# One TensorE loop body per unit, with the spread of v as an inner loop, in an attention-times-value kernel

## The chip, the cores and the metric

The kernel runs on one core of a Trainium2 chip. The metric is device time in microseconds (us) of one execution, given as the median of several runs. The engines of the core are TensorE (PE; its weight loads are listed apart as PEld), VectorE (DVE), ScalarE (ACT), GpSimd (POOL) and SyncE (SP). Sixteen DMA engines move data between the chip's memory and the on-chip memories; here GpSimd issues most transfers and SyncE a few.

## What is computed

```
batch, n_heads, seq, head_dim = 8, 12, 1024, 64
np.einsum('bhqs,bhsd->bhqd', attn_weights, v).astype(np.float32)
```

There are 96 heads. For each one, a 1024 x 1024 matrix of attention weights is multiplied with a 1024 x 64 matrix v. Inputs and output are float32. The attention weights alone are 402.7 MB, so nearly all of the traffic is reading them once.

## The kernel before

**Units.** Four heads are taken together (24 such groups, `NV`), and a group's attention weights come in two loads of 1024 x 2048 values, called units here (48, `NU`). GpSimd's DMA converts a unit to bf16 while it loads it into one of two buffers `abf[0]` and `abf[1]`: even units (i = 0) into the first, odd units into the second. A buffer is free for the next load but one as soon as TensorE has transposed its content.

**What TensorE does for a unit**, in this order (`pe_unit`, line 199):

- Transposes (`transpose_g`, line 139, recorded as L144): 16 groups `g` of four 128 x 128 transposes; two bf16 values travel as one float32 word. They go through four banks of the accumulation memory, and VectorE (10 of 16 groups) and ScalarE (6 of 16) copy them to `at` (`copy_g`, L277). A group waits for the copy of the group four before it (`s_cp`).
- Spread, for even units only (`spread_v`, line 154, L161): the four heads' v lies in `vr` with rows over partitions, eight heads on 128 partitions, 16 partitions each. Matmuls with a 0/1 matrix `spread` bring it into the layout that the product needs: for each of the four heads, eight matmuls of 512 columns are summed in one bank. The operands are slices of 32 partitions (`rows`), and two heads whose slices differ are interleaved. Four copies of this code exist, one for each place that a group can have in `vr`, and three nested tests choose one. VectorE and ScalarE cast two banks each to `vbf` (`spread_copy`, L250).
- Transposing back (`transpose_back`, line 171, L174) of the product of the unit before, from `ot`; ScalarE copies it to the output buffer `osb` (`back_copy`, L258).
- Product (`multiply`, line 184, L189): for each of four heads and two halves, eight matmuls that accumulate `vbf` times `at`. VectorE and ScalarE copy the result to `ot` (`product`, L289).

TensorE's loop runs 24 times, and its body holds both units of a group, each written out, plus the four copies of the spread. After the loop one more transposing back is written out.

**What sets the order.** Every engine runs its instructions in program order, and engines wait for each other by semaphores with counts worked out by hand. GpSimd's queue is a fixed list: for each unit n it waits until all transposes of n are done (`s_t[True]` at line 396; the last group, 15, is one of VectorE's) and issues the load of unit n + 2. Ahead of some even units it waits until a spread is done (`s_sp`, line 394) and issues a load of v for the next groups; the attention load behind it in the list then waits too. Stores of finished output are issued by GpSimd in two bursts (`BURSTS`, after groups 8 and 16), twice at its end, and three times by SyncE at the end; SyncE also passes on, through `s_half`, that a burst has been stored or that the second half of one of the last two units has landed. Those last two units are loaded in halves. TensorE looks at `s_half` ahead of group 8 of each unit.

Of the kernel before, what the change touches and what calls it, by code (L numbers as in the profile page):

```python
# [10 lines left out]
def kernel(  # L11
# [76 lines left out]
    def count_of(g):  # L88

        return sum(on_dve(x) == on_dve(g) for x in range(g + 1))  # L90

    PER_DVE = sum(on_dve(g) for g in range(G))
    PER_ACT = G - PER_DVE

# [15 lines left out]
    bank = [nc.alloc_psum_tensor(f"bank{i}", [P, 512], fp32).ap() for i in range(8)]  # L110
    pt = [b.rearrange("p (k j) -> p k j", k=KW) for b in bank[:4]]
    po = bank[4:6]
    px = bank[6:8]

# [7 lines left out]
    s_t = {True: sem("s_t_dve"), False: sem("s_t_act")}  # L122
# [4 lines left out]
    s_last, s_ot, s_vbf = sem("s_last"), sem("s_ot"), sem("s_vbf")  # L127
# [8 lines left out]
    with tc.tile_critical(sync_engine=mybir.EngineType.Pool, no_gpsimd_drain=True):  # L136
        pe = nc.tensor

        def transpose_g(a, g, n):
            if g >= 4:  # L140
                pe.wait_ge(s_cp[g - 4], n)
            words = a[:, g].bitcast(fp32).rearrange("p (c k) -> p k c", k=KW)
            for k in range(KW):
                last = pe.matmul(  # L144
                    out=pt[g % 4][:, k],
                    lhsT=words[:, k],
                    rhs=ident,
                    is_transpose=True,
                    start=(k == 0),
                    stop=(k == KW - 1),  # L150
                )
            last.then_inc(s_t[on_dve(g)])

        def spread_v(n, banks):

            for pair in ((0, 2), (1, 3)):
                for b in range(VB):
                    for h in pair:
                        j = n % 2 * VH + h
                        rows = ds(j * (P // V8) // VR * VR, VR)  # L160
                        last = pe.matmul(  # L161
                            out=banks[h],
                            lhsT=spread[rows, j, ds(VB - 1 - b, P)],
                            rhs=vr[rows, n // 2, b],
                            start=(b == 0),
                            stop=(b == VB - 1),
                        )
                        if b == VB - 1:
                            last.then_inc(s_sp)

        def transpose_back():
            for j0 in range(0, GH, 4):
                for j in range(4):
                    last = pe.matmul(  # L174
                        out=px[j0 // 4][:, ds(j * P, P)],
                        lhsT=ot[:, j0 + j],
                        rhs=ident,
                        is_transpose=True,
                        start=(j == 0),
                        stop=(j == 3),  # L180
                    )
                last.then_inc(s_back)

        def multiply(outs, h, half):

            n = 0
            for kw in range(KW):
                for par in range(2):
                    last = pe.matmul(  # L189
                        out=outs,  # L190
                        lhsT=vbf[:, 2 * kw + par, h],
                        rhs=at[:, ds(half * GH, GH), kw, ds(h * VP, VP), par],
                        start=(n == 0),
                        stop=(n == SB - 1),
                    )
                    n += 1
            return last

        def pe_unit(i, n, both, loaded, it):

            pe.wait_ge(*loaded)
            for g in range(G):
                if g == GH:
                    pe.wait_ge(s_half, n)
                transpose_g(abf[i], g, n)
            pe.wait_ge(s_ot, both)
            if i == 0:
                pe.wait_ge(s_vr, it)
                which = pe.snap((it - 1) % V_AT_ONCE)
                with pe.If(which > 1):  # L210
                    with pe.If(which > 2):
                        spread_v(3, po + px)
                    with pe.Else():
                        spread_v(2, po + px)
                with pe.Else():
                    with pe.If(which > 0):
                        spread_v(1, po + px)
                    with pe.Else():
# [3 lines left out]
            pe.wait_ge(s_last, both)  # L222
            for hp in range(2):
                for h in range(2):
                    for half in range(2):
                        outs = po[hp][ds(half * D, D), ds(h * GH * VP, GH * VP)]
                        last = multiply(outs, 2 * hp + h, half)
                last.then_inc(s_m)

        pe.wait_ge(s_const, 4)  # L230
        with nc.Fori(1, NV + 1, 1, engines=(PE,)) as it:
            loaded = pe.snap(it * 16)
            second = pe.snap(it * 2)
            first = pe.snap(second - 1)
            both = pe.snap(it * 4)
# [230 lines left out]
```

## Time and profile before

| quantity | value |
|---|---|
| median of 3 runs | 1050.6 us (1050.5 to 1050.88) |
| the profiled execution's own time | 1050.13 us |
| its span, from first to last instruction | 1048.7 us |
| mean granted TensorE clock | 0.876 |
| read from and written to the chip's memory | 427.82 MB and 25.17 MB |
| transposes (L144), PE busy | 430.3 us of 3072 matmuls |
| product (L189), PE busy | 226.3 us of 3072 matmuls |
| spread (L161), PE busy | 87.0 us of 768 matmuls |
| transposing back (L174), PE busy | 61.9 us of 392 matmuls |
| PE idle before transposes, until a load of attention weights | 186.5 us |
| loads of attention weights, of a whole unit | 46, median 29.4 us from issue to landing |
| loads of v of 2048 KB | 5, median 15.7 us from issue to landing |

A page of the profile gives each engine's busy time, the span in 40 slices with the share of time that the DMA engines moved data, the groups of equal instructions with busy time, mean duration and the idle time ahead of them, and the chain of waits that ended last. Asked for a stretch of time, the trace gives the same figures for that stretch, or the instructions in order (the timeline). Sizes of loads are those written on the chip, in bf16, half of what is read. Busy time on an engine that others wait for counts; idle time on an engine that nobody waits for costs nothing.

### The profile page before, as it was taken

The numbers are of one execution on the slowest core, as the hardware profiler recorded it, in microseconds if no ns is written. First come the engines' busy times: TensorE is split into PE (matmuls) and PEld (weight loads), VectorE is DVE, ScalarE is ACT, GpSimd is POOL, SyncE is SP. The second block draws the span as 40 slices with busy tenths as digits, with TensorE's granted clock in tenths as the row PEclk, the third lists the DMA queues.
The fourth block names the chain that finished last, engine by engine and source line by source line (L and its number), as shares of the span: only waits on it lengthen the run. The fifth ranks groups of instructions, "written<-read, shape, count | busy, mean of one in ns | idle before, by whom it ended". The sixth has DMA issues, their size and how long they took to land.

```text
span 1048.7 us, 17363 instructions
## 1 busy us (share of the span) xinstructions
PE 795.5 (76%) x7304; PEld 708.5 (68%) x7304; DVE 389.4 (37%) x584; ACT 469.5 (45%) x590; POOL 36.9 (4%) x68
## 2 busy tenths in 40 slices
PE   0978789479889493888949789858577784988994
PEld 0777688368778383777848678657567674877883
DVE  1443344234435151343415344324234332433542
ACT  0445355344545261354536355344335443545553
POOL 1000000000000000000000000000000000000000
PEclk9989799798999696889879889889878987888997
DMA  9999999999999999999999999999999999999999
GB/s 216 226 219 219 216 212 215 220 219 217 220 215 209 220 220 376 220 217 211 211 224 220 216 220 212 210 221 220 318 238 217 212 210 224 220 216 219 209 214 402
DMA packets 10662, 239.68 MB, mean 229 GB/s; under 512 B 1056, under 2 KB 1056, under 8 KB 1184
## 3 DMA queue, kind: packets, MB, share of 16 engines
q0 software_dynamic: 10080, 232.26, 98.9%
q1 hardware_dynamic: 576, 7.34, 1.7%
q8 instruction: 3, 0.05, 0.0%
q14 instruction: 3, 0.02, 0.0%
HBM read 427.82 MB, written 25.17 MB: 432 GB/s over the span
## 4 chain that ended last, share of the span: by engine, by line
DMA 71%; PE 26%; issue 1%; POOL 1%; ACT 0%; DVE 0%; ACTq 0%; SPq 0%; POOLq 0%
DMA abf<-in_attn_weights_dram 63%; PE bank L144 22%; DMA out_dram<-osb 8%; PE bank L161 3%; PE bank L189 1%; PE bank L174 0%; POOL vr L350 0%; ACT osb L258 0%; DVE osb L258 0%; ACT vbf L250 0%; POOL abf L344 0%; ACT ot L289 0%; POOL out_dram L358 0%; ACTq L258 0%; SPq L420 0%
## 5 line engine op out<-in xcount | busy, mean ns | idle before, releaser
L144 PE MATMUL bank<-ident,abf 128*128 128x128 f32 x3072 | 430.3, 307 | 210.1 <-DMA abf<-in_attn_weights_dram 186.5
L144 PEld LDWEIGHTS bank<-ident,abf 128*128 128x128 f32 x3072 | 420.4, 212 | 221.9 <-DMA abf<-in_attn_weights_dram 193.8
L277 DVE COPY at<-bank 128x1024 bf16<-128x1024 bf16 x480 | 319.7, 689 | 400.1 <-PE bank L144 397.9
L277 ACT COPY at<-bank 128x1024 bf16<-128x1024 bf16 x288 | 287.8, 1012 | 327.2 <-PE bank L144 327.2
L189 PE MATMUL bank<-at,vbf 128*64 128x256 bf16 x3072 | 226.3, 286 | 0.0
L189 PEld LDWEIGHTS bank<-at,vbf 128*64 128x64 bf16 x3072 | 204.1, 111 | 19.6 <-issue 6.3
L258 ACT COPY osb<-bank 64x512 f32 (+1 forms) x194 | 112.4, 580 | 28.2 <-PE bank L174 25.7
L289 DVE COPY ot<-bank 128x512 f32<-128x512 f32 x48 | 33.2, 691 | 208.6 <-PE bank L189 208.6
L161 PE MATMUL bank<-vr,spread 32*128 32x512 bf16 x768 | 87.0, 375 | 0.5 <-issue 0.2
L289 ACT COPY ot<-bank 128x512 f32<-128x512 f32 x48 | 28.1, 585 | 130.5 <-PE bank L189 130.5
L174 PE MATMUL bank<-ident,ot 128*128 128x128 f32 x392 | 61.9, 309 | 29.4 <-ACT vbf L250 28.7
L174 PEld LDWEIGHTS bank<-ident,ot 128*128 128x128 f32 x392 | 50.8, 158 | 41.5 <-ACT vbf L250 40.5
L161 PEld LDWEIGHTS bank<-vr,spread 32*128 32x128 bf16 x768 | 35.3, 93 | 43.7 <-issue 1.6
L250 ACT CAST vbf<-bank 128x512 bf16<-128x512 f32 x48 | 25.8, 588 | 74.3 <-PE bank L161 74.3
L344 POOL DMA_DIRECT2D abf<-in_attn_weights_dram x50 | 26.9, 538 | 813.2 <-PE bank L144 812.3
L250 DVE CAST vbf<-bank 128x512 bf16<-128x512 f32 x48 | 30.9, 686 | 29.0 <-PE bank L161 29.0
L277 ACT ACT_TABLE_LOAD x12 | 15.4, 1283 | 6.5 <-DMA osb<-in_v_dram 6.3
L350 POOL DMA_DIRECT2D vr<-in_v_dram x6 | 4.0, 674 | 134.5 <-PE bank L161 134.5
L358 POOL DMA_DIRECT2D out_dram<-osb x5 | 3.1, 619 | 7.5 <-ACT osb L258 7.5
L325 DVE MEMSET ident<- 128x128 f32 x1 | 0.2, 165 | 6.3 <-DMA osb<-in_v_dram 6.3
L258 DVE COPY osb<-bank 64x512 f32<-64x512 f32 x2 | 1.4, 689 | 3.0 <-PE bank L174 3.0
L332 DVE CAST vr<-osb 128x1024 bf16<-128x1024 f32 x2 | 2.2, 1137 | 0.0
(9 smaller groups left out, 5.1 us busy)
## 6 DMA issues: line engine op xcount, KB each, us to landing
abf<-in_attn_weights_dram POOLq DMA_DIRECT2D x46, 4096.0 KB, 29.4
vr<-in_v_dram POOLq DMA_DIRECT2D x5, 2048.0 KB, 15.7
out_dram<-osb POOLq DMA_DIRECT2D x1, 8192.0 KB, 39.3
abf<-in_attn_weights_dram POOLq DMA_DIRECT2D x4, 2048.0 KB, 23.4
out_dram<-osb POOLq DMA_DIRECT2D x3, 2048.0 KB, 34.1
out_dram<-osb SPq DMA_DIRECT2D x3, 2048.0 KB, 14.3
out_dram<-osb POOLq DMA_DIRECT2D x1, 4096.0 KB, 42.8
osb<-in_v_dram SPq DMA_DIRECT2D x1, 1024.0 KB, 5.2
```

What stands on the lines that cost most here:

```text
L144: last = pe.matmul(out=pt[g % 4][:, k], lhsT=words[:, k], rhs=ident, is_transpose=True, start=(k == 0), stop=(k == KW - 1),)
L161: last = pe.matmul(out=banks[h], lhsT=spread[rows, j, ds(VB - 1 - b, P)], rhs=vr[rows, n // 2, b], start=(b == 0), stop=(b == VB - 1),)
L174: last = pe.matmul(out=px[j0 // 4][:, ds(j * P, P)], lhsT=ot[:, j0 + j], rhs=ident, is_transpose=True, start=(j == 0), stop=(j == 3),)
L189: last = pe.matmul(out=outs, lhsT=vbf[:, 2 * kw + par, h], rhs=at[:, ds(half * GH, GH), kw, ds(h * VP, VP), par], start=(n == 0), stop=(n ...
L250: copy(out=vbf[:, :, h], in_=ps.rearrange("p (k d) -> p k d", k=SB)).then_inc(s_vbf)
L258: last = copy(out=rows[ds(n // 2 % 2 * HP, HP), ds(pp * 2 * G + n % 2 * G, G)].rearrange("p (half j) d -> p j half d", half=2)[:, ds(4 * k ...
L277: ins = copy(out=at[:, g].rearrange("c k j two -> c (k j two)"), in_=bank[g % 4].bitcast(bf16),)
L289: copy(out=ot.rearrange("c j (pp h p) -> c h j pp p", pp=2, h=VH)[:, ds(2 * e, 2)], in_=po[e].rearrange("c (h j p pp) -> c h j pp p", h=2, ...
L332: last = nc.vector.tensor_copy(out=vr_first[:, 0, part], in_=v32[:, part])
L344: pool.dma_start(out=abf[n % 2][:, ds(g0, gn)].rearrange("p g s -> p (g s)"), in_=attn_q[n // 2][:, ds((n % 2 * G + g0) * S, gn * S)],).th ...
L350: pool.dma_start(out=vr[:, ds(q % V_AT_ONCE // 2, fours // 2)].rearrange("p n b x -> p n (b x)"), in_=v_n(q, fours),).then_inc(s_v, 16)
L358: eng.dma_start(out=out_n(q, fours), in_=at_slot, **({"single_packet": True} if eng is pool and fours == 2 else {}),).then_inc(done, 16)
```

## The change

TensorE's loop now runs 49 times, once for each unit and one more (`step`). A step has the product of the unit before, then the transposes of its own unit (written out twice, for the two buffers, behind a test), after even units' transposes the spread, and then the transposing back. So product and transposing back exist once in the program, and the last ones are done in the extra step, where a test leaves out the transposes.

The spread is an inner loop over the four heads. Its operands are no longer slices of 32 partitions but all 128, with zeros in `spread` for the rows of other heads, and the addresses are worked out from the loop's register. The heads come one after another instead of two interleaved.

The banks of the accumulation memory are one tensor so that a register can choose one. The semaphores that counted by engine (`s_t`, `s_last`, `s_ot`, `s_vbf`) now count by bank or by one engine each, and increments of two make all counts advance by four a unit, so that one base register serves all waits of VectorE and ScalarE. The waits for the earlier results (`s_ot`, `s_vr`) sit on the last matmuls of an even unit's transposes, the wait for `s_half` one matmul earlier than before. VectorE's loop holds two units instead of four. GpSimd's list has the same transfers in the same order, waiting for the same events with other counts.

The core of the diff:

```diff
-        def spread_v(n, banks):
-
-            for pair in ((0, 2), (1, 3)):
+        def spread_v(j0, part):
+            with nc.Fori(0, VH, 1, engines=(PE,)) as h:
                 for b in range(VB):
-                    for h in pair:
-                        j = n % 2 * VH + h
-                        rows = ds(j * (P // V8) // VR * VR, VR)
-                        last = pe.matmul(
-                            out=banks[h],
-                            lhsT=spread[rows, j, ds(VB - 1 - b, P)],
-                            rhs=vr[rows, n // 2, b],
-                            start=(b == 0),
-                            stop=(b == VB - 1),
-                        )
-                        if b == VB - 1:
-                            last.then_inc(s_sp)
+                    last = pe.matmul(
+                        out=bank[:, ds(h + 4, 1)].rearrange("p one x -> p (one x)"),
+                        lhsT=spread[:, ds(h + j0, 1), ds(VB - 1 - b, P)].rearrange(
+                            "p one x -> p (one x)"
+                        ),
+                        rhs=vr[:, ds(part, 1), b].rearrange("p one x -> p (one x)"),
+                        start=(b == 0),
+                        stop=(b == VB - 1),
+                    )
+                last.then_inc(s_sp, 2)
...
+        def step(it):
+            with pe.If(it > 1):
+                multiply(it)
+            with pe.If(it < NU + 1):
+                with pe.If(pe.snap(it % 2) < 1):
+                    pe.wait_ge(s_abf[1], pe.snap(it * 8))
+                    transposes(1, it)
                 with pe.Else():
-                    with pe.If(which > 0):
-                        spread_v(1, po + px)
-                    with pe.Else():
-                        spread_v(0, po + px)
-                pe.wait_ge(s_vbf, it * 4)
-            transpose_back()
...
+                    pe.wait_ge(s_const, 4)
+                    pe.wait_ge(s_abf[0], pe.snap(it * 8 + 8))
+                    transposes(0, it)
+                    spread_v(pe.snap(it // 2 % 2 * VH), pe.snap(it // 4 % 2))
+                    for e in range(2):
+                        pe.wait_ge(s_vbf[e], it)
+            for e in range(2):
+                pe.wait_ge(s_ot[e], it)
+            transpose_back()
+
+        with nc.Fori(1, NU + 2, 1, engines=(PE,)) as it:
+            step(it)
...
                 if n % 2 == 0:
-                    spread_copy(e, po[e], of_sp + (2 * n + 2 * e + 2))
-                    spread_copy(2 + e, px[e], of_sp + (2 * n + 2 * e + 2))
+                    spread_copy(e, po[:, e], now[2 * e + 2])
+                    spread_copy(2 + e, px[:, e], now[2 * e + 6]).then_inc(s_vbf[e], 2)
...
-                pool.wait_ge(s_sp, 4 * (q + 1))
+                pool.wait_ge(s_sp, 8 * (q + 1))
                 load_v(q + 1, V_LOADS[q + 1])
-            pool.wait_ge(s_t[True], (n + 1) * PER_DVE)
+            pool.wait_ge(s_t[3], 4 * (n + 1))
             load_attn(n + 2)
```

How TensorE's instructions stand at the spread of an even unit, before: the tests, and the first two of the four written-out copies, each closed by a branch.

```order
L210 ISA [waits s_vr,s_ot]
L210 COMPARE_AND_BRANCH
L211 COMPARE_AND_BRANCH
L161 MATMUL bank<-vr,spread 128x512 x32
L211 UNCONDITIONAL_BRANCH
L161 MATMUL bank<-vr,spread 128x512 x32
L213 UNCONDITIONAL_BRANCH
```

And now, at the head and at the end of the inner loop; `ISA` rows load registers for the addresses, and the rows between these two pieces repeat the pair of `ISA` and `MATMUL`.

```order
L142 MATMUL bank<-ident,abf 128x128 [waits s_vr]
L153 UNCONDITIONAL_BRANCH
L153 ISA
L155 ISA x2
L155 MATMUL bank<-vr,spread 128x512
L155 ISA
```

```order
L153 REGISTER_ALU
L153 COMPARE_AND_BRANCH
L204 UNCONDITIONAL_BRANCH [waits s_vbf1,s_vbf0]
L169 MATMUL bank<-ident,ot 128x128 [waits s_ot1,s_ot0]
L169 MATMUL bank<-ident,ot 128x128 x7
L215 REGISTER_ALU
L215 COMPARE_AND_BRANCH
```

The 32 matmuls of a spread became eight that are passed through four times, with a register instruction ahead of each, and a branch now stands between the spread and the transposing back, as well as one behind the latter.

TensorE again, at the product. Before, it stood between the transposing back and the next unit's transposes, with nothing else between them:

```order
L174 MATMUL bank<-ident,ot 128x128 x7
L189 MATMUL bank<-at,vbf 64x256 [waits s_last]
L189 MATMUL bank<-at,vbf 64x256 x63
L144 MATMUL bank<-ident,abf 128x128 [waits s_abf1]
```

Now it stands at the head of the loop's body:

```order
L198 COMPARE_AND_BRANCH
L187 MATMUL bank<-at,vbf 64x256 x7
L187 MATMUL bank<-at,vbf 64x256 [waits s_last0]
L187 MATMUL bank<-at,vbf 64x256 [waits s_last1]
L187 MATMUL bank<-at,vbf 64x256 x55
L198 UNCONDITIONAL_BRANCH
L200 COMPARE_AND_BRANCH
L201 REGISTER_ALU
L201 COMPARE_AND_BRANCH
L202 REGISTER_ALU
L142 MATMUL bank<-ident,abf 128x128 [waits s_abf1]
```

The order of product and transposes is the same; the loop's back branch and a test moved between transposing back and product, and further tests between product and transposes.

More of the change, by code (lines that the diff above doesn't have):

```diff
@@ L120 @@
     s_held = sem("s_held")
-    s_t = {True: sem("s_t_dve"), False: sem("s_t_act")}
+    s_t = [sem(f"s_t{b}") for b in range(4)]
     s_sp, s_m = sem("s_sp"), sem("s_m")
@@ L137 @@
         pe = nc.tensor
[L139 to L150, printed above, removed]
-                )
-            last.then_inc(s_t[on_dve(g)])
@@ L181, in transpose_back @@
                     )
[L182 to L197, printed above, removed]
```

128 lines of the change are left out of this document (65 added, 63 removed).

## The prediction

> **What bounds the kernel now.** I read the page first, then the share of the DMA engines over the long middle stretch, then one pair of units on TensorE, then when GpSimd issues loads. On the page:
>
> ```profile
> span 1048.7 us, 17363 instructions
> PE 795.5 (76%) x7304; PEld 708.5 (68%) x7304; DVE 389.4 (37%) x584; ACT 469.5 (45%) x590; POOL 36.9 (4%) x68
> DMA  9999999999999999999999999999999999999999
> q8 instruction: 3, 0.05, 0.0%
> DMA 71%; PE 26%; issue 1%; POOL 1%; ACT 0%; DVE 0%; ACTq 0%; SPq 0%; POOLq 0%
> ```
>
> No slice of the 40 shows the 16 DMA engines below nine tenths, while TensorE is idle for a quarter of the span. The chain of waits names PE for 26%, but that is transposition time between a landing and the next issue, during which the other load is still moving. The table by stretch, asked for one stretch from the first transfers to the last store (its next to last figure is the DMA share, the last GB/s), says the same without slices:
>
> ```profile
> 2.50:1046.00 1043.50, 795.53 (x7304) 708.50 (x7304) 389.39 (x584) 469.49 (x590) 35.50 (x63) 0.88 1.01 229
> ```
>
> A share of 1.01 over 1043.5 us leaves nothing to win between those two times: the bytes are the same after the change, so a faster TensorE cannot shorten this stretch, and a slower one costs time only where a transfer is issued after the queue ahead of it has emptied. So the prediction is a sum of leads. A plain pair of units on TensorE (timeline: start, duration, line, idle before):
>
> ```profile
> 545.70 9.31 PE L144 MATMUL bank<-ident,abf 128*128 128x128 f32 x64 [14.04 <-DMA abf<-in_attn_weights_dram]
> 555.06 3.63 PE L161 MATMUL bank<-vr,spread 32*128 32x512 bf16 x32
> 559.88 1.09 PE L174 MATMUL bank<-ident,ot 128*128 128x128 f32 x8 [1.20 <-ACT vbf L250]
> 560.91 4.48 PE L189 MATMUL bank<-at,vbf 128*64 128x256 bf16 x64
> 565.32 7.95 PE L144 MATMUL bank<-ident,abf 128*128 128x128 f32 x64
> 573.10 1.04 PE L174 MATMUL bank<-ident,ot 128*128 128x128 f32 x8
> 574.07 4.48 PE L189 MATMUL bank<-at,vbf 128*64 128x256 bf16 x64
> 584.31 5.89 PE L144 MATMUL bank<-ident,abf 128*128 128x128 f32 x27 [5.76 <-DMA abf<-in_attn_weights_dram]
> ```
>
> From one even unit's landing to the next is 584.31 - 545.70 = 38.6 us. TensorE works until 574.07 + 4.48 = 578.55, so 32.85 us, and then waits 5.76 us. GpSimd's issues around a pair with a load of v, and the landing times of two of them, each asked for by a window that holds one issue (the last figure is us from issue to landing):
>
> ```profile
> 488.73 0.53 POOL L344 DMA_DIRECT2D abf<-in_attn_weights_dram  x1 [19.14 <-PE bank L144]
> 510.62 0.70 POOL L350 DMA_DIRECT2D vr<-in_v_dram  x1 [21.36 <-PE bank L161]
> 511.31 0.56 POOL L344 DMA_DIRECT2D abf<-in_attn_weights_dram  x1
> 573.57 0.53 POOL L344 DMA_DIRECT2D abf<-in_attn_weights_dram  x1 [17.73 <-PE bank L144]
> ...
> abf<-in_attn_weights_dram POOLq DMA_DIRECT2D x1, 4096.0 KB, 27.9
> ```
>
> The load issued at 488.73 lands at 516.6. What follows it in the queue (v, then the next even load) is issued at 510.62, a lead of 6.0 us. In a plain pair the odd load, issued at 573.57, has the even one ahead of it until 584.3: a lead of 10.7 us.
>
> **The spread, part by part.** Before, 32 matmuls of 32 rows run in pairs on two row groups. Their weight loads and matmuls (ns, least, median, most), and the page's row of the transposes' weight loads (mean 212 ns):
>
> ```profile
> L161 PEld LDWEIGHTS bank<-vr,spread x768: 91/93/95, 35.5 to 1012.0; 32*128 32x128 bf16 x192
> L161 PE MATMUL bank<-vr,spread x768: 374/374/387, 35.5 to 1012.2; 32*128 32x512 bf16 x192
> ...
> L144 PEld LDWEIGHTS bank<-ident,abf 128*128 128x128 f32 x3072 | 420.4, 212 | 221.9 <-DMA abf<-in_attn_weights_dram 193.8
> ```
>
> One takes 0.374 us and 32 end in 3.63, so a pair follows a pair after (3.63 - 0.374) / 15 = 0.217 us. After the change each matmul uses all 128 rows, so none has a partner: 31 x 0.217 + 0.374 = 7.1 us, that is 3.5 us more. The loop adds sequencer work: per turn nine ISA instructions, one register step and one branch beside eight matmuls. The nearest rows are TensorE's own branch at the loop's end and, from the chain of waits, ScalarE's register instructions ahead of copies with computed addresses:
>
> ```profile
> L231 PEldq COMPARE_BRANCH  x24: 67/208/222, 60.0 to 1032.2; - x24
> ...
> 378.49 0.05 ACTq L258
> 378.53 0.05 issue
> 378.58 0.05 ACTq L258
> ```
>
> Such an instruction comes about every 0.1 us with what it dispatches, a branch takes 0.21 and some 0.06 around it. A turn is then 9 x 0.1 + 0.1 + 0.27 = 1.27 us plus the dispatch of eight matmuls and loads; L189's 64 in 4.48 us bound that by 8 x 0.07 = 0.56, together 1.83 us against 8 x 0.217 = 1.74 us in the array. Bounds: 7.1 us where the queue hides the sequencer; 32 x (0.374 + 0.093) = 14.9 us where nothing overlaps. I take four turns of 1.83, 7.3 us, since L144 and L189, also without partners, run pipelined: **+3.7 us**. The Trainium skill ("TensorE: Matmul & The Clock Gate", section on packing small matmuls) states that weight loads overlap running matmuls only where the row group differs, which speaks against full-height matmuls: by it the sum would be 32 x 0.093 = 3.0 us more. The trace disagrees for L144, where 64 full-height loads of 0.212 us each, 13.6 us in all, fit in 7.95 us.
>
> **The rest on TensorE.** The wait after the spread (1.20 us) held both ScalarE casts; now one of ScalarE's two can run while the last bank is filled, which takes off about half of it, and a branch that carries the waits gives about as much back: between -0.5 and +0.3, I take -0.1. The product now stands behind the loop's back branch and a test, so between transposing back and product the sequencer has a register step and two branches, 0.1 + 2 x 0.27 = 0.64 us, of which TensorE's 1.04 us of transposing back covers over half: 0 to 0.6, I take +0.25 for each unit. The tests ahead of the transposes lie behind the 4.48 us of product and cost nothing; without that cover three branches and steps would be 1.0 us. The Trainium skill ("Runtime: NRT & Kernel Launch", instruction fetch mechanics) warns that a taken branch out of the loaded window stalls on a fetch. Here 24 back branches take at most 0.222 us and the instruction queue carried three packets in all, so that price is left at zero.
>
> Sum for a pair: 3.7 - 0.1 + 2 x 0.25 = **+4.1 us**, 36.95 us of 38.6. TensorE still finishes 1.7 us before the next landing, so the sum is not passed on. Besides, with 1.7 us of idle instead of 5.76 the first transposes may run at the 7.95 us of the pair's fifth row instead of 9.31, up to 1.4 us back. The odd load moves from 573.57 to about 577.4, still 6.9 us ahead of 584.3. The issue of the even load follows its transposes and does not see the spread.
>
> VectorE's loop of two units, the semaphores per bank, and the wait for the second half one matmul earlier change no duration; their cover is VectorE's and ScalarE's idle time (63% and 55% of the span). If it were gone, one VectorE branch per pair would cost about 0.3 us.
>
> **Loads of v (six).** Here GpSimd waits for the spread itself, and the next even load stands behind it in GpSimd's order. The delay is +3.7 us, or 2.3 if the transposes before it run faster; the lead is 6.0 us, less the time from issue to first byte. That start-up has two bounds (queue and issue rows, then stretches with DMA share and GB/s):
>
> ```profile
> 0.74 0.38 SPq L134 DMA_DIRECT2D osb<-in_v_dram  x1
> 1.33 0.67 POOL L344 DMA_DIRECT2D abf<-in_attn_weights_dram  x1 [0.89 <-POOLq L450]
> ...
> 0.00:1.70 1.70, 0.00 (x0) 0.00 (x0) 0.00 (x0) 0.00 (x0) 0.57 (x5) 1.00 0.00 0
> 1.70:2.70 1.00, 0.00 (x0) 0.00 (x0) 0.00 (x0) 0.00 (x0) 1.00 (x3) 1.00 0.96 188
> 2.70:4.70 2.00, 0.00 (x0) 0.00 (x0) 0.00 (x0) 0.00 (x0) 0.38 (x1) 1.00 0.95 377
> 4.70:6.00 1.30, 0.00 (x0) 0.00 (x0) 0.00 (x0) 0.00 (x0) 0.00 (x0) 1.00 2.07 485
> ```
>
> SP's queue moves bytes 1.0 us after its issue at 0.74. GpSimd's load, issued at 1.33, shows beside it from 4.7 on at the latest, so at most 3.4 us. I take the middle, 2.2: 3.7 + 2.2 = 5.9 of 6.0 us. Nothing is lost, by 0.1 us; at 3.4 it is 1.1 us each, at 1.0 nothing.
>
> **The end.** TensorE was late here already (timeline; then the last store's issue, its landing after 11.7 us, and the DMA share at the end):
>
> ```profile
> 966.18 10.52 PE L144 MATMUL bank<-ident,abf 128*128 128x128 f32 x64 [4.38 <-DMA abf<-in_attn_weights_dram]
> 1000.06 4.11 PE L144 MATMUL bank<-ident,abf 128*128 128x128 f32 x32
> 1004.93 4.12 PE L144 MATMUL bank<-ident,abf 128*128 128x128 f32 x32 [0.76 <-SPq L426]
> 1024.26 4.11 PE L144 MATMUL bank<-ident,abf 128*128 128x128 f32 x32 [0.91 <-SPq L426]
> ...
> 1036.88 0.33 SPq L358 DMA_DIRECT2D out_dram<-osb  x1
> out_dram<-osb SPq DMA_DIRECT2D x1, 2048.0 KB, 11.7
> 1043.00:1046.00 3.00, 0.00 (x0) 0.00 (x0) 0.00 (x0) 0.00 (x0) 0.00 (x0) 0.50 1.00 426
> 1046.00:1048.70 2.70, 0.00 (x0) 0.00 (x0) 0.00 (x0) 0.00 (x0) 0.00 (x0) 0.50 0.41 176
> ```
>
> The last store's 2 MB at 426 GB/s are 4.9 us, and bytes end near 1046.0 + 0.41 x 2.7 = 1047.1, so its own begin near 1042.2; with 1.0 us of start-up it may be issued until 1041.2, a lead of 4.3 us. The delay on the way: 4.1 us from the pair at 966.18, or 1.6 if its transposes drop from 10.52 to about 8; 0.76 us of it vanishes in the wait at 1004.93, 3.85 us are added by the last spread, 0.91 us vanish at 1024.26, and 0.5 us come from two more branches. That gives 4.3 to 6.8 us against 4.3: a loss between 0 and 2.5 us. I take 0.8, nearer the lower end, because the idle time before 966.18 falls from 4.38 to 0.3 us and every transposition that followed at once took 7.95.
>
> Total: the profiled execution's 1050.13 + 0 + 0.8 = 1050.9 us; that execution lies 0.5 us below the median of 1050.6, so **1051.4 us** on the medians' scale. A difference under 0.2% (2.1 us) I count as none.
>
> **Rivals.** *Loads of v come late* (slower): the start-up is nearer 3.4 than 2.2 us, or a turn of the loop nearer 2.3 than 1.83. It decides from a sum of delay and start-up above 6.0 us. At 3.4 us six loads lose 1.1 each, 6.6 us; at turns of 2.3 us, 1.8 us each, with the larger loss at the end: 1053 to 1063, about 1057 us. For it speaks that 5.9 of 6.0 us are used up, against it that the transposes ahead may shorten by 1.4 us. *Weight loads do not overlap at full height*: the 3.0 us more make the pair 39.95 us, about 38.6 with fast transposes; each load of v then loses 6.7 + 2.2 - 6.0 = 2.9 us less up to 1.4, and the end some 4: about 1067 us. L144's rows speak against it. *TensorE becomes the bound*: at 14.9 us for the spread a pair is 44.5 us, 43.2 with fast transposes, 4.6 us too many in each of 18 pairs without a load of v: about 1133 us. Against it: L144's and L189's pitch. *Faster*: only the ends outside 2.5 to 1046 us could give, some 2 us, about 1048 us; the order of the DMA issues there is unchanged, so little speaks for it.
>
> **The numbers.** Hidden, within 0.2%: 0.54, by itself 1050.2 to 1052.7. Late v loads and end: 0.32. No overlap of weight loads: 0.07. TensorE as the bound: 0.03. Faster by over 0.2%: 0.04. Slower is 0.32 + 0.07 + 0.03 = 0.42. The range 1050.2 to 1060 takes in the first case and most of the second.
>
> **What would show it.** The spread group should rise from 24 x 3.63 = 87 us busy to 24 x 7.3 = 175 us, with 128 rows per matmul; each v load should be issued some 2 to 4 us later against the load ahead of it; TensorE's idle time for loads should shrink by 65 to 100 us (24 x 4.1, less what faster transposes give back); and the DMA share should stay at 1.0. A stretch with the share below 1 right after an issue of v, or ahead of the last store, proves the second case; TensorE without any wait for loads in plain pairs proves the bound wrong.

## The result, and the profile after

The changed kernel took 1063.38 us (median of 4 runs, 1062.02 to 1064.86) against 1050.74 us (4 runs, 1050.5 to 1050.88): 1.0122 times the time before, with a 95% interval of 1.011 to 1.0135. That is 12.6 us more, where 0.8 us more was forecast.

The page of the changed kernel, in the lines that were shown of the kernel before:

```profile
span 1063.4 us, 18205 instructions
PE 826.5 (78%) x7208; PEld 711.2 (67%) x7304; DVE 391.1 (37%) x584; ACT 471.7 (44%) x590; POOL 37.0 (3%) x68
DMA  9999999999999999999899999999999999999999
q8 instruction: 1, 0.02, 0.0%
DMA 67%; PE 29%; issue 2%; POOL 0%; ACT 0%; DVE 0%; ACTq 0%; SPq 0%; POOLq 0%
...
L155 PE MATMUL bank<-vr,spread 128*128 x672 | 160.7, 379 | 34.4 <-issue 32.0
```

The last line is the group of the spread's matmuls, with 32.0 us of idle time that is new (a part of it holds matmuls that the trace did not record, as worked out below). Otherwise next to nothing on this page says where the time went. The row of the DMA engines has one digit of 40 that is an 8, and TensorE still idles for a fifth of the span. The losses are stretches of one to three microseconds, and a slice is 27 us wide. They show only in windows chosen by hand. The next table gives stretches of the changed kernel around the fourth load of v, which is issued at 522.08 (columns: stretch, length, busy time of TensorE, its weight loads, VectorE, ScalarE and GpSimd, granted clock, DMA share, GB/s):

```profile
517.00:521.00 4.00, 3.11 (x15) 1.44 (x16) 0.69 (x1) 0.59 (x1) 0.00 (x0) 1.00 0.84 180
521.00:523.40 2.40, 1.21 (x8) 0.62 (x7) 0.00 (x0) 0.59 (x1) 1.25 (x2) 1.00 0.07 14
523.40:526.00 2.60, 2.60 (x36) 2.38 (x36) 0.00 (x0) 2.24 (x4) 0.00 (x0) 1.00 0.96 161
```

The middle row is a hole, but its last two figures need care. This table counts a packet whole in the stretch in which it starts (a packet is one piece of a transfer; in a load of attention weights it has 32 KB and takes 2.43 us). So 0.07 and 14 GB/s say that hardly a packet starts in these 2.4 us, while packets that started earlier still run out in them. Counted by the time for which packets run, the 16 engines are busy for 0.33 of that stretch, and between 521 and 526 they lose 1.95 us each on the mean. The same place in the kernel before, between the landing of the load ahead and the bytes of v:

```profile
515.00:517.40 2.40, 2.40 (x45) 2.34 (x41) 0.69 (x1) 0.08 (x1) 0.00 (x0) 1.00 0.95 198
```

Here packets go on starting without a break, and by running time the share is 1.03. GpSimd's issues around that load in the changed kernel (start, duration, line, and in brackets the wait before):

```profile
499.29 0.53 POOL L320 DMA_DIRECT2D abf<-in_attn_weights_dram  x1 [22.18 <-PE bank L142]
522.08 0.71 POOL L326 DMA_DIRECT2D vr<-in_v_dram  x1 [22.27 <-PE bank L155]
522.78 0.56 POOL L320 DMA_DIRECT2D abf<-in_attn_weights_dram  x1
```

It waits for L155, the spread, as before. On TensorE's timeline the spread is now four groups, one for each turn of the inner loop (columns as above):

```profile
67.02 9.43 PE L142 MATMUL bank<-ident,abf 128*128 128x128 f32 x64 [3.53 <-DMA abf<-in_attn_weights_dram]
...
505.69 7.95 PE L142 MATMUL bank<-ident,abf 128*128 128x128 f32 x64 [1.42 <-DMA abf<-in_attn_weights_dram]
...
513.79 1.67 PE L155 MATMUL bank<-vr,spread 128*128 x7 [0.15 <-issue]
515.88 1.67 PE L155 MATMUL bank<-vr,spread 128*128 x7 [0.41 <-issue]
518.00 1.67 PE L155 MATMUL bank<-vr,spread 128*128 x7 [0.45 <-issue]
520.11 1.67 PE L155 MATMUL bank<-vr,spread 128*128 x7 [0.44 <-issue]
522.98 1.06 PE L169 MATMUL bank<-ident,ot 128*128 128x128 f32 x8 [1.20 <-ACT vbf L226]
523.97 4.48 PE L187 MATMUL bank<-at,vbf 128*64 128x256 bf16 x64
```

A turn is 2.11 us: 1.67 for the seven matmuls that the trace has of its eight (672 are recorded of 768), and 0.44 in which the array looks idle. The missing one is the first of each turn: the semaphore that the last one raises goes up at 515.48, just where the seventh recorded one ends (513.79 + 1.67 = 515.46). So about half of the 0.44 us holds a matmul. Eight at the spacing of 0.216 us that experiment 5 shows are 1.73 us, so a turn takes 0.38 us more than its matmuls need. From the start of the spread to the transposing back are 522.98 - 513.79 = 9.19 us, where it was 559.88 - 555.06 = 4.82.

**Where the 14.7 us of the two profiled executions lie.** (The profiled execution of the changed kernel was the longest of its four, 1064.86 us.) A landing is recorded apart for each of the 16 DMA queues that share a load. With the mean over the 16 for every load in order, after minus before, the difference grows in steps, and between the steps it moves by less than 0.5 us from one landing to the next:

```
place                                  growth of the difference, us
the six loads of v                     2.2  1.0  1.5  2.6  1.8  0.9   = 9.9
the attention load ahead of a burst    1.3  1.45                      = 2.7
the last store                         1.4
all other landings together            about 1.5
```

The sum is 15.6 us for the mean of the 16 queues, and 14.7 for the last of them (1048.60 to 1063.35); of the last store's 1.4 only 0.2 show in its last landing. The pairs without a load of v, three quarters of the kernel, cost next to nothing.

### The profile page after: what moved, and what is told of

Its sections match the earlier page's. It is cut to its first block, busy times and chain, and to the rows that moved or that the text cites. A ratio compares the mean times of both kernels' runs of the same rounds, so it can differ in the third digit from the quotient of the medians.

```text
span 1063.4 us, 18205 instructions
## 1 busy us (share of the span) xinstructions
PE 826.5 (78%) x7208; PEld 711.2 (67%) x7304; DVE 391.1 (37%) x584; ACT 471.7 (44%) x590; POOL 37.0 (3%) x68
## 4 chain that ended last, share of the span: by engine, by line
DMA 67%; PE 29%; issue 2%; POOL 0%; ACT 0%; DVE 0%; ACTq 0%; SPq 0%; POOLq 0%
DMA abf<-in_attn_weights_dram 60%; PE bank L142 21%; DMA out_dram<-osb 8%; PE bank L155 6%; PE bank L187 2%; PE bank L169 1%; POOL vr L326 0%; ACT vbf L226 0%; ACT osb L234 0%; DVE osb L234 0%; ACT ot L265 0%; POOL abf L320 0%; POOL out_dram L334 0%; ACTq L234 0%; ACTq L225 0%
## 5 line engine op out<-in xcount | busy, mean ns | idle before, releaser
L142 PE MATMUL bank<-ident,abf 128*128 128x128 f32 x3072 | 408.2, 297 | 166.2 <-DMA abf<-in_attn_weights_dram 139.4
L142 PEld LDWEIGHTS bank<-ident,abf 128*128 128x128 f32 x3072 | 398.7, 211 | 177.4 <-DMA abf<-in_attn_weights_dram 145.4
L187 PE MATMUL bank<-at,vbf 128*64 128x256 bf16 x3072 | 215.1, 278 | 0.0
L187 PEld LDWEIGHTS bank<-at,vbf 128*64 128x64 bf16 x3072 | 196.7, 108 | 13.4 <-issue 8.0
L155 PE MATMUL bank<-vr,spread 128*128 x672 | 160.7, 379 | 34.4 <-issue 32.0
L155 PEld LDWEIGHTS bank<-vr,spread 128*128 x768 | 74.6, 97 | 113.4 <-issue 50.5
L226 ACT CAST vbf<-bank 128x512 bf16<-128x512 f32 x48 | 28.1, 586 | 169.6 <-PE bank L155 169.6
L226 DVE CAST vbf<-bank 128x512 bf16<-128x512 f32 x48 | 33.2, 692 | 112.5 <-PE bank L155 112.5
L169 PE MATMUL bank<-ident,ot 128*128 128x128 f32 x392 | 51.5, 274 | 28.6 <-ACT vbf L226 27.9
L169 PEld LDWEIGHTS bank<-ident,ot 128*128 128x128 f32 x392 | 43.4, 141 | 40.0 <-issue 40.0
```

The costliest lines, as they stand in the source:

```text
L142: last = pe.matmul(out=pt[g % 4][:, k], lhsT=words[:, k], rhs=ident, is_transpose=True, start=(k == 0), stop=(k == KW - 1),)
L155: last = pe.matmul(out=bank[:, ds(h + 4, 1)].rearrange("p one x -> p (one x)"), lhsT=spread[:, ds(h + j0, 1), ds(VB - 1 - b, P)].rearrange ...
L169: last = pe.matmul(out=px[:, j0 // 4, ds(j * P, P)], lhsT=ot[:, j0 + j], rhs=ident, is_transpose=True, start=(j == 0), stop=(j == 3),)
L187: last = pe.matmul(out=po[ds(half * D, D), h // 2, ts(h % 2, GH * VP)], lhsT=vbf[:, 2 * kw + par, h], rhs=at[:, ds(half * GH, GH), kw, ds( ...
L226: return copy(out=vbf[:, :, h], in_=ps.rearrange("p (k d) -> p k d", k=SB))
```

## The experiments

The theories, as the expectations name them. **A**: time is lost where the load of v is issued too late before its queue runs dry. **B**: TensorE's longer work itself is the cost, through its own chain of landing, transposes and next issue. **C**: the prediction's way of counting holds, so that a load of v loses only what the lead to the last landing lacks of the start-up, and the time went somewhere else.

**1. The kernel before, with GpSimd held back by some 3 us.** One wait more ahead of the loads of v; TensorE's program is untouched.

```diff
                 pool.wait_ge(s_sp, 4 * (q + 1))
+                pool.wait_ge(s_back, 2 * (n + 1))
                 load_v(q + 1, V_LOADS[q + 1])
```

> The kernel before, with one wait more on GpSimd: a load of v goes out only when the transposing back behind the spread is done, about 3.1 us after the spread's end. TensorE's code is untouched. Theory A (the time is lost where a load of v, and the attention load behind it, is issued too short before the queue runs empty; the changed kernel's own rows give a loss of 0.9 us plus what the issue lacks to 1.75 us ahead of the mean landing): the issue stands 5.05 - 3.1 = 2 us ahead, 0.9 to 1.5 us lost six times, 1056 to 1060 us. Theory B (TensorE's own longer work sets the time, the v loads are no cause): no change, 1050.7 us. Theory C (the prediction's way of counting: nothing is lost as long as the issue comes more than the start-up of 1.4 us ahead of the last landing, here 6.0 - 3.1 = 2.9 us): no change, 1050.7 us.

Measured: 1062.65 us (1059.9 to 1065.29) against 1050.42, ratio 1.0124 (1.0107 to 1.0141). The fourth load of v, in GpSimd's timeline of this kernel, now follows the transposing back:

```profile
519.89 0.71 POOL L350 DMA_DIRECT2D vr<-in_v_dram  x1 [26.35 <-PE bank L174]
```

The delay alone, with the spread at its old 3.63 us, costs nearly as much as the whole change. B and C fall. The median lies above A's range. In the profiled execution (1059.9 us, the shortest of the four) the six loads of v lose 6.2 us, as A has it, and two losses that A does not contain come on top: 1.4 and 1.1 us at the attention loads ahead of the two bursts of stores, as in the changed kernel. Where the longer executions lost more, no trace shows.

**2. The same with some 5 to 7 us.**

```diff
                 pool.wait_ge(s_sp, 4 * (q + 1))
+                pool.wait_ge(s_m, 2 * n + 1)
                 load_v(q + 1, V_LOADS[q + 1])
```

> As the run before it, but the load of v waits for the first half of the product, about 5.4 us after the spread's end, so the issue stands about 0.3 us behind the mean landing. Theory A: 0.9 + 2.1 = 3 us lost six times, 16 to 20 us, 1067 to 1071 us. Theory B: 1050.7 us. Theory C: 0.6 us ahead of the last landing against a start-up of 1.4, 0.8 us six times, about 1056 us.

Measured: 1073.27 us (1072.03 to 1074.44), ratio 1.0213 (1.0196 to 1.023). Stretches of this kernel around the fourth load of v, issued at 528.53 (columns as above):

```profile
526.00:528.00 2.00, 2.00 (x34) 1.88 (x32) 0.00 (x0) 0.36 (x1) 0.00 (x0) 0.90 0.01 0
528.00:530.00 2.00, 2.00 (x29) 1.75 (x26) 0.69 (x1) 0.06 (x1) 1.25 (x2) 1.00 0.14 16
530.00:532.00 2.00, 2.00 (x18) 2.00 (x19) 1.11 (x2) 1.42 (x2) 0.00 (x0) 1.00 0.98 164
```

Hardly a packet starts for 4 us; by running time the share is 0.56, 0.01 and 0.95 in the three stretches, and 3.0 us are lost. TensorE is busy throughout: its work is not what fails, the issue is. A again: the six loads lose 20.8 us, where A has 16 to 20, and with 2.5 us at the bursts the time lies above its range.

**3. The changed kernel, with the loads of v made early.** Groups are fetched by two instead of four, and GpSimd waits for a spread two groups back, which has long been done.

```diff
-    V_LOADS = {2: 2, **{q: V_AT_ONCE for q in range(V_AT_ONCE, NV, V_AT_ONCE)}}
+    V_LOADS = {q: 2 for q in range(2, NV, 2)}
...
-                pool.wait_ge(s_sp, 8 * (q + 1))
+                if q > 1:
+                    pool.wait_ge(s_sp, 8 * (q - 1))
```

> The changed kernel, with v loaded in eleven pieces for two groups each, and GpSimd waiting only for the spread two groups earlier, so each load of v is issued before the transposes and no issue waits for a spread that is just running. Theory A: the 9.9 us that the six loads of v cost in the changed kernel (steps of the mean landing) come back, 1053 to 1055 us; what stays is 2.7 us at the two bursts of stores and about 1.5 us at the last store. Theory B: no gain, 1062 to 1064 us.

Measured: 1051.22 us (10 runs, 1050.77 to 1052.35) against 1050.42, ratio 1.0009 (1.0 to 1.0019). GpSimd's timeline and the middle stretch of this kernel:

```profile
490.62 0.53 POOL L320 DMA_DIRECT2D abf<-in_attn_weights_dram  x1 [22.13 <-PE bank L142]
491.14 0.54 POOL L326 DMA_DIRECT2D vr<-in_v_dram  x1
```

```profile
2.50:1046.00 1043.50, 828.84 (x7208) 713.56 (x7304) 391.40 (x584) 471.20 (x590) 37.15 (x68) 0.94 1.01 228
```

The load of v goes out right behind an attention load, with no wait of its own, and the DMA share is back at 1.01, although TensorE has the full-height rows, the inner loop and 33 us more of recorded work than the kernel before. A's mechanism is right; it expected more time because it left the losses at the bursts in, and they vanished too. What remains, 0.8 us, appears at the last store. The mean landing of the store ahead of it is still that of the kernel before (1042.95 and 1042.87); its own comes 1.5 us later (1049.18 and 1047.72), its last landing 0.65 (1049.25 and 1048.60).

**4. The changed kernel with the old spread.** Four written-out copies, 32 rows, two heads interleaved; all else of the change stays.

```diff
-        def spread_v(j0, part):
-            with nc.Fori(0, VH, 1, engines=(PE,)) as h:
+        def spread_v(n):
+            for pair in ((0, 2), (1, 3)):
                 for b in range(VB):
...
+                    for h in pair:
+                        j = n % 2 * VH + h
+                        rows = ds(j * (P // V8) // VR * VR, VR)
...
-                    spread_copy(e, po[:, e], now[2 * e + 2])
+                    spread_copy(e, po[:, e], now[4 * e + 4])
...
```

> The changed kernel, with the spread as before: slices of 32 partitions, two heads interleaved, four copies written out behind tests, no inner loop. All else of the change stays. Theory A: the spread falls back to 3.6 us and with it every delay, 1050 to 1052 us. If the rest of the change (one loop body for both units, the product behind the back branch, VectorE's loop of two units) costs time of its own, 1055 us or more.

Measured: 1050.45 us against 1050.42, ratio 1.0 (0.9991 to 1.001), and the spread on TensorE's timeline of this kernel is what it was:

```profile
506.83 3.63 PE L158 MATMUL bank<-vr,spread 32*128 32x512 bf16 x32
```

One loop body for all units, VectorE's loop of two units and all the other new branches and counts cost nothing that shows. The whole loss comes through the spread's duration.

**5. The kernel before with full-height rows and no inner loop.** This parts the two edits of the spread.

```diff
-                        rows = ds(j * (P // V8) // VR * VR, VR)
+                        rows = ds(0, P)
```

> The kernel before, with the one change that each matmul of the spread uses all 128 rows; the spread stays written out four times, without a loop, and the heads stay interleaved. Theory A: 31 x 0.217 + 0.374 = 7.1 us instead of 3.63, so each v load is issued up to 3.5 us later, 1.5 to 3 us ahead of the mean landing, 0.9 to 1.2 us lost six times, and 0 to 2.7 us at the bursts: 1056 to 1060 us, most of the loss of the changed kernel. If the inner loop alone is the cause, 1050.4 us with the spread still near 3.6 us or hidden.

Measured: 1060.52 us (4 runs, 1056.9 to 1060.78) against 1050.47, ratio 1.0085 (1.0066 to 1.0104). The spread's groups in this kernel, and one instance on TensorE's timeline:

```profile
L161 PE MATMUL bank<-vr,spread 128*128 128x512 bf16 x750 | 167.9, 379 | 1.4 <-issue 0.2
L161 PEld LDWEIGHTS bank<-vr,spread 128*128 128x128 bf16 x768 | 73.7, 98 | 87.7 <-issue 1.6
```

```profile
562.71 7.08 PE L161 MATMUL bank<-vr,spread 128*128 128x512 bf16 x31
```

A spread takes 7.08 us with 32 weight loads of 98 ns in it. That is the 7.1 us of the matmuls alone, and not some 3 us more, so the loads lie under the matmuls before them. The rule of the Trainium skill ("TensorE: Matmul & The Clock Gate", section "Part 3: Packing small matmuls — row/col tiling"), that a weight load overlaps only where the row group differs, does not hold for these full-height matmuls. The time is just above A's range. The full-height rows alone, at which a single matmul takes the 0.216 us that a pair took before, cost 10.0 of the 12.6 us by the medians (6.4 in the shortest of the four runs). The rest is left for the inner loop, which makes each spread another 1.1 us longer; no run has the loop alone.

**The bursts.** Ahead of each burst of stores the last packets of an attention load took 2.9 to 4.1 us in place of 2.4, on all 16 queues, in the changed kernel and in experiments 1, 2 and 5, and not in 3 and 4 (3 has three packets of 2.7 to 3.1 us near the second burst). **D**: it comes from a late issue of the load right behind the burst. **E**: one late load of v leaves the queues in a state that lasts. **F**: it comes when the load of v one pair ahead of the burst was late.

**6. The kernel before, with only the attention load behind a burst held back.**

```diff
             load_attn(n + 2)
...
+            if i == 1 and q in BURSTS:
+                pool.wait_ge(s_m, 2 * n + 2)
```

> The kernel before, where the one load of attention weights that follows each burst of stores waits for the product too, about 5.5 us longer. In the changed kernel the last packets ahead of both bursts took 3.5 to 4.1 us instead of 2.43 on all 16 queues, 1.3 and 1.5 us lost. Theory D (the late issue of this load disturbs the transfer that is running): such packets here too, 2.7 us, 1053.1 us. Theory E (it comes only once the queue has run short earlier on, whatever the issue here): no slow packet, 1050.4 us.

Measured: 1050.53 us, ratio 1.0 (0.9991 to 1.001). At the first burst four packets of 2.7 to 2.9 us, none at the second: D falls.

**7. The kernel before, with only the first load of v late** (the wait of experiment 2 under `if q == 1`, far ahead of any burst).

```diff
+                if q == 1:
+                    pool.wait_ge(s_m, 2 * n + 1)
```

> The kernel before, with only the first of the six loads of v made late, as in the run with 5.4 us. That load cost 4.8 us there. Theory E (a queue that has run short once stays in another state, and each burst of stores then loses 1.3 us): 4.8 + 2.6 = 7.4 us, 1057 to 1058.5 us, with slow packets ahead of both bursts, 300 and 650 us later. Theory D, or any theory by which each place pays for itself: 4.8 us, 1055 to 1055.5 us, without slow packets there.

Measured: 1054.94 us (1054.39 to 1055.37) against 1050.47, ratio 1.0044 (1.0027 to 1.0061). The step at that load is 4.4 us, and neither burst has a slow packet: E falls. One late load is one loss, and nothing later wins it back.

**8. The kernel before, with only the third load of v late**, the one a pair ahead of the first burst.

```diff
+                if q == 7:
+                    pool.wait_ge(s_m, 2 * n + 1)
```

> The kernel before, with only the third load of v made late (by the 5.4 us of the product's first half); it is the last one ahead of the first burst of stores. Theory F (slow packets come ahead of a burst when the load of v one pair earlier was late): the load itself 2 to 4 us, 16 packets of over 2.7 us ahead of the first burst, 1.3 us, none ahead of the second: 1053.7 to 1055.7 us. If late loads of v only pay for themselves: no such packets, 1052.4 to 1054.4 us. The profile decides, more than the time.

Measured: 1054.38 us (1053.37 to 1056.48) against 1050.45, ratio 1.0044 (1.0027 to 1.0061). The step at the load is 2.3 us; another 1.1 comes ahead of the first burst, none at the second. The stretch ahead of that burst in this kernel:

```profile
380.00:398.00 18.00, 18.00 (x200) 17.11 (x200) 8.01 (x12) 10.71 (x15) 1.29 (x2) 0.96 1.01 217
398.00:402.00 4.00, 0.36 (x4) 0.09 (x1) 0.00 (x0) 0.58 (x1) 0.00 (x0) 1.00 0.88 131
```

The same in the changed kernel, and then in the kernel before:

```profile
401.00:405.00 4.00, 4.00 (x52) 3.77 (x51) 1.45 (x3) 3.34 (x6) 0.54 (x1) 1.00 0.93 131
405.00:409.00 4.00, 2.16 (x34) 1.84 (x29) 0.69 (x1) 0.59 (x1) 0.00 (x0) 1.00 1.01 422
```

```profile
398.00:402.00 4.00, 1.36 (x7) 1.36 (x8) 0.19 (x1) 0.00 (x0) 0.00 (x0) 0.60 0.77 328
```

With a late load of v the packets that start in 4 us carry 131 GB/s, although the share reads 0.88 and 0.93. The load's last 16 packets take 3.1 to 3.9 us each here, and 3.4 to 4.0 in the changed kernel, in place of 2.43; a slow packet counts as a busy engine, so only the last column shows the loss. In the kernel before, the stores' rate follows at once. The time alone fits both theories' ranges, but the slow packets stand where F has them, at the first burst and not at the second. What in the chip slows those packets stays open; no run here tells it.

**9. The kernel before with early loads of v**, the edit of experiment 3.

```diff
-                pool.wait_ge(s_sp, 4 * (q + 1))
+                if q > 1:
+                    pool.wait_ge(s_sp, 4 * (q - 1))
```

> The kernel before with v in eleven pieces, each issued ahead of the transposes without waiting for a running spread (as tried on the changed kernel). Theory A: its queue was never short, so there is nothing to win, 1050 to 1050.9 us. If the loads of v cost something even in the kernel before, up to 3 us less, 1047.5 to 1049.5 us.

Measured: 1050.54 us, ratio 1.0001 (0.9991 to 1.001). Before the change the queue was never short, and there was nothing to win; the smaller pieces cost nothing either. Experiment 3 changed the size and the time of the loads together; that its gain comes from the time rests on experiments 1 and 2. No version tried is faster than the kernel before; experiments 4, 6 and 9 equal it.

## Why the prediction was wrong

**What failed is the step "Nothing is lost, by 0.1 us" for the loads of v.** Its inputs held at five of the six loads, its yardstick at none. The delay: by the last landing of the load ahead, the lead at the fourth load fell from 6.0 to 524.97 - 522.08 = 2.9 us, that is by 3.1, inside the predicted 2.3 to 3.7 (from the second load to the sixth it fell by 2.3 to 3.1). The start-up, which the prediction took at 2.2, is 1.4: the first packet of the load issued at 522.08 starts at 523.51, and two other loads of v give the same. By the prediction's own sum, 3.1 + 1.4 = 4.5 of 6.0 us, there was 1.5 us to spare, and still 2.6 us were lost. The 6.0 us had been read from one landing time, the last queue's. TensorE starts on that last landing, so GpSimd's issue is tied to the slowest queue, while each of the 16 queues runs dry by itself. Here they finish from 521.48 to 524.97: the earliest is empty 0.6 us before v is even issued. In stretches of 0.4 us from 520.8 on, the 16 engines run packets for 0.99, 0.61, 0.37, 0.25, 0.18 and 0.07 of the time. The lead to the mean landing was 0.1 us, not 2.9; in the kernel before it was 5.05. It fell by 5.0 and not by 3.1 because the queues had also drifted apart: the last landing lay 2.8 us behind the mean, and 0.9 before the change.

At the first load of v, where they were still together, the delay was enough: it was 4.4 us, not 3.7 or 2.3, which left 1.4 of 5.8 us to the last landing. The first packet came 1.2 us after the issue, so the prediction's way of counting still had nothing lost; 2.2 us were.

Put against that lead, the losses of all kernels line up (us; lead from the issue of v to the mean landing of the load ahead, and the step at that load, which holds both what the queue idles and the slower first packets):

```
kernel                lead : loss, for the loads of v that were delayed
changed kernel        0.42:2.2  2.55:1.0  1.30:1.5  0.08:2.6  0.69:1.8  2.53:0.9
5, full-height rows   0.99:1.8  2.55:1.0  2.45:1.1  1.50:1.2  1.88:1.0  2.38:0.3
1, late by 3          2.53:0.9  1.67:1.2  0.80:1.6  1.69:0.95 1.33:1.2  3.25:0.3
2, late by 5 to 7    -2.16:4.8 -1.21:3.6  0.57:1.95 -1.13:3.6 -0.76:3.25 -1.16:3.65
7 and 8, one late    -1.67:4.4  0.25:2.3
kernel before         4.3 to 5.1 : 0, at all six
6, shortest lead      3.99 : 0
```

Up to a lead of about 1.5 us the loss is 2.5 us less the lead, within 0.4 us; from there to 2.5 us a loss near 1 us remains in most cases; at 4 us there is none. The 2.5 us can be read apart from it: the five loads of v of 2048 KB in experiment 2, whose first packets came when all queues were empty, land on the mean 12.1 to 12.2 us after their issue, and in the kernel before such a load lands 9.7 us after the load ahead (515.67 to 525.40). So the 2.2 us that the prediction took were not far off as a price, though too much as a time to the first packet. What failed was the point to count from: with the lead of 5.05 us to the mean landing in place of 6.0, its own sum of 5.9 us would have given a loss of 0.85 us at each load.

The rival "Loads of v come late", to which a chance of 0.32 was given, was this mechanism, with the wrong point from which it decides and too small a price. It asked for a start-up near 3.4 us, or for a turn of the loop nearer 2.3 than 1.83 us; the turn came out at 2.11, so this second sign held. By its own sum a turn of 2.11 is a loss of 1.0 us a load, and the mean loss was 1.65. The time came out just above its 1053 to 1063.

**The bursts**: no term of the prediction held their 2.7 us. They follow from the late loads of v, as experiments 3 and 8 show.

**The end**: 0.8 us was taken from a span of 0 to 2.5. The step there is 1.4 us of the mean landing in the changed kernel and 0.2 of the last one, and experiment 3, which has nothing but the late end, lies 0.8 us above the kernel before. The stretches before the last store, as the prediction asked for:

```profile
1056.00:1058.50 2.50, 0.00 (x0) 0.00 (x0) 1.09 (x2) 0.44 (x1) 0.00 (x0) 0.73 0.42 177
1058.50:1062.00 3.50, 0.00 (x0) 0.00 (x0) 0.00 (x0) 0.00 (x0) 0.00 (x0) 0.50 1.05 449
```

The share falls to 0.42 (0.47 by running time) while the store waits for the last copies: right in place, and near in size, in part by luck. The delay against the store ahead was 6.1 us, toward the upper end of the 4.3 to 6.8; and the lead of 4.3 was too small, because the share of 0.41 at the end of the kernel before counts packets by their start: bytes ended at 1048.6 and not near 1047.1.

**The spread**: 7.3 us were predicted, 3 x 2.11 + 1.67 plus the unrecorded matmul's 0.2 give 8.2, so this term was 0.9 us too small. The matmuls' pitch was right (7.1 predicted without the loop, 7.08 measured in experiment 5). The sequencer's share was too small, as these rows of the changed kernel show (ns, least, median, most):

```profile
L155 PEldq FUSED_REGOPS  x864: 69/74/195, 34.9 to 1033.1; - x173
...
L153 PEldq FUSED_REGOPS  x96: 114/116/126, 34.7 to 1031.5; - x96
L153 PEldq COMPARE_BRANCH  x96: 76/208/232, 36.6 to 1033.4; - x96
```

The branch of 0.21 us was taken rightly, but it was counted into a sum that the array's time was to hide. The array does run out of work at each of the three back branches: branch, register steps and the first weight load stand one behind another, and 0.38 us of it shows in each turn of 2.11 us.

**The rest of TensorE's sum**: the wait after the spread went from 1.20 to 1.2 (-0.1 predicted), and the product follows the start of the transposing back by 523.97 - 522.98 = 1.0 us as before, so the +0.25 for each unit did not come. The pair grew by 9.19 - 4.82 + 0.15 = 4.5 us, 4.1 predicted. As foreseen, transposes after a shorter idle gap fall to 7.95 us: at 505.69, by the row above, after 1.42 us. At the same place in the kernel before the gap was 3.59 us:

```profile
497.31 9.42 PE L144 MATMUL bank<-ident,abf 128*128 128x128 f32 x64 [3.59 <-DMA abf<-in_attn_weights_dram]
```

The granted clock over these two groups was 1.00 and 0.82. At 67.02 the gap was still 3.53 us and the transposes stayed at 9.43, so there the full delay of 4.4 us reached the load of v, and its lead to the last landing was 1.4 and not 2.9 us.

**The bound**: right. Plain pairs cost nothing, and TensorE waits for loads in them still. That idle time fell from 186.5 to 139.4 us, by 47 and not by the 65 to 100 that were named: 24 x 4.5 = 108 us came in, but transposes, product and transposing back got shorter by 22, 11 and 10 us (the mean granted clock was 0.933, and 0.876 before), and the span grew by 15. The rival without overlap of weight loads and the rival with TensorE as the bound are refuted by experiment 5 and by the DMA share of 1.01 in experiment 3.

## What to carry to other kernels

When the DMA engines are the bound, a change to a compute engine costs what it delays the issues. Check each issue against the mean of the 16 landings of the load ahead, or the first of them, not against the last, which is the landing that the page gives. In this kernel a lead of 4 us to the mean was safe, and 2.5 us mostly was not. Where such a lead is short, move the issue, not the work: with the loads of v made early, 4.5 us more work for each spread cost 0.8 us in all.

## What the hardware showed beside this

- An issue that comes before the queues are empty can still be too late: with 2.4 to 2.6 us of lead, more than the 1.4 us from issue to first packet, the mean landing came 0.9 to 1.1 us late in five of six cases (0.3 in the sixth). The first packets behind the restart at 523.5 mostly took 0.9 to 1.4 us, those of an undisturbed load of v 0.62.
- The last landing hides losses. At the fifth load of v the last queue's landing did not move against the load before it, while the mean of the 16 moved by 1.8 us: the queues that were ahead gave up their advance, and the span paid later.
- The last 16 packets of the attention load ahead of a burst of stores took 2.9 to 4.1 us in place of 2.43 in every run in which the load of v one pair earlier was late, and in none of the others (experiments 3 and 6 have three and four slower ones, of 2.7 to 3.1); the cause is open.
- A loop of eight matmuls with addresses from registers lost 0.38 us of TensorE's time at each back branch: a turn of 2.11 us against 8 x 0.216 = 1.73. Fetching the instructions cost nothing that shows: the instruction queue carried one packet, three before.
